# Interleaving the last Exp and Ln halves of a prefix log-sum-exp scan, and storing the tile above the last in two column halves

## The chip, the cores and the metric

The kernel runs on one core of a Trainium2 chip. The metric is the device time in microseconds (us) of one execution of the whole program. Before the change it is 1255.22 us, the median of six executions (1253.7 to 1270.8).

## What is computed

The input `x` has the shape 8 x 4096 x 2048 in float32. Along the middle axis a running log-sum-exp is taken, for each of the 8 batches and each of the 2048 columns by itself:

```
out[:, 0, :] = x[:, 0, :]
for t in range(1, S):
    mx = maximum(out[:, t-1, :], x[:, t, :])
    out[:, t, :] = mx + log(exp(out[:, t-1, :] - mx) + exp(x[:, t, :] - mx))
```

This is log(cumulative sum of exp(x)). Input and output have 268.44 MB each, and every byte crosses between HBM and the core once.

## The kernel before

**Tiles.** The 4096 rows of a batch are cut in 8 blocks (NBLK) of 512 rows, so there are 64 tiles (NT), each of 512 rows x 2048 columns, 4 MB. A tile lies in the core's memory as 128 partitions x 4 rows (R) x 2048 columns: partition p holds the four consecutive rows 4p to 4p+3, which are 32 KB in one piece in HBM. There are four input buffers `ti` and two output buffers `to`. Every tile is worked on in two column halves of 1024 columns, h = 0 and h = 1. Below, "Exp 63/0" is the Exp of tile 63, column half 0, and so on.

**Stages of a tile.** (1) SyncE loads the tile into `ti` (L114). (2) ScalarE takes Exp in place, one instruction for each half (L133). (3) VectorE adds each row of a partition to the one after it, three additions for each half (`local`, L248). (4) TensorE multiplies the last rows with a triangle of ones, which gives each partition the sum of all partitions above it (`triangle`, L224, two matmuls for each half into PSUM). (5) VectorE adds that sum to all four rows (`join`, L257, one instruction for each half). (6) TensorE starts the sum of the next tile from the last row of this one (`carry`, L213, two matmuls for each half); the last tile of a batch has no next one, and only a semaphore is passed on. (7) ScalarE takes Ln (L140), one instruction for each half, which waits for the carry of that half. (8) ScalarE's queue issues the store (L165 in the loop, L177 in the tail).

**The order of the work** is written out by hand for each engine; nothing is scheduled by a planner, and each engine executes its own list in order, waiting on semaphores. VectorE's order for each tile is local/0, local/1, join/0, join/1. TensorE's is triangle/0, triangle/1, carry/0, carry/1. SyncE loads tile n+4 into a buffer once both Ln halves of tile n have been taken from it (`freed`). ScalarE's list is a software pipeline: the Exp halves of tile n stand before the Ln halves of tile n-1. A loop covers tiles 0 to 59. The tail, written out after it (L182 to L198), covers the Exp of tiles 61 to 63 and the Ln and the stores of tiles 60 to 63. In the tail Ln works in place in `ti`, and the store leaves from there. All stores of the tail add to one semaphore, `final`, and the last instruction of ScalarE waits for all of them.

**The place that is changed** is the last turn of that tail (n = 63, so `up` = 62):

```
else:
    ln(up, 0, up - first, True)
    exp(n, 0)
    ln(up, 1, up - first, True)
    finals += store(up)
    exp(n, 1)
```

ScalarE thus executes Ln 62/0, Exp 63/0, Ln 62/1, the store of the whole tile 62, Exp 63/1, and then (L196 to L198) Ln 63/0, store 63/0, Ln 63/1, store 63/1. `exp(n, 0)` first takes the semaphore of the tile's load (L132), and whatever stands behind it on ScalarE waits with it. `store(n, h)` waits until that Ln has completed and issues one DMA; with h given, it moves one column half, whose pieces in HBM are 4 KB (one row of 1024 columns) and not 32 KB.

Of the kernel before, what the change touches and what calls it, by code (L numbers as in the profile page):

```python
# [9 lines left out]
def kernel(  # L10
# [29 lines left out]
    NT = B * NBLK  # L40
# [16 lines left out]
    def half(h):  # L57
        return slice(h * HALF, (h + 1) * HALF)

    def event(engine, waits, updates):  # L60

        engine.add_instruction(mybir.InstEventSemaphore(  # L62
            name=f"I-{nc.next_id()}", engine=engine.engine, ins=[], outs=[],
            sync_info=mybir.SyncInfo(
                on_wait=[mybir.SyncWait(
                    sync_type="semaphore", id=s.num, ant_name=s.name,
                    wait_mode="sem-ge-imm", wait_value=n,
                ) for s, n in waits],
                on_update=[mybir.SyncUpdate(
                    sync_type="semaphore", id=s.num, ant_name=s.name,  # L70
                    update_mode=mode, update_value=n,
                ) for s, mode, n in updates],
            ),
        ))

    def take(engine, s, n):

        event(engine, [(s, n)], [(s, "sem-sub-imm", n)])

    with tc.tile_critical():  # L80
# [12 lines left out]
        with nc.Block() as block:  # L93

            @block.gpsimd
            def _(g):
                g.memset(before[:], 1.0).then_inc(ones, 1)  # L97
                g.memset(last[:], 1.0).then_inc(ones, 1)  # L98
                g.wait_ge(ones, 2)

                g.affine_select(  # L101
                    out=before[:], in_=before[:], compare_op=mybir.AluOpType.is_ge, fill=0.0,
                    base=-1, pattern=[[1, P]], channel_multiplier=-1,
                ).then_inc(shaped, 1)

                g.affine_select(  # L106
                    out=last[:], in_=last[:], compare_op=mybir.AluOpType.is_ge, fill=0.0,
                    base=-(P - 1), pattern=[[0, P]], channel_multiplier=1,
                ).then_inc(shaped, 1)
# [17 lines left out]
            @block.scalar  # L127
            def _(act):
                def exp(n, h, rows=slice(0, R)):
                    t = ti[n % NI]  # L130
                    if h == 0:
                        take(act, loaded[n % NI], 16)  # L132
                    act.activation(  # L133
                        t[:, rows, half(h)], t[:, rows, half(h)], ACT.Exp
                    ).then_inc(exps[h], 1)

                def ln(n, h, turn, in_place=False):
                    if h == 0 and not in_place:
                        take(act, stored[n % NO], 16)
                    act.activation(  # L140
                        (ti[n % NI] if in_place else to[n % NO])[:, :, half(h)],
                        ti[n % NI][:, :, half(h)], ACT.Ln,
                    )._wait_ge(carried[h], turn + 1).then_inc(logs, 1)

                def settle(turns):
                    take(act, carried[0], turns)
                    take(act, carried[1], turns)
                    take(act, logs, 2 * turns)

                for n in range(NO):  # L150
                    act.sem_inc(stored[n], 16)
                take(act, top, 16)
                act.activation(ti[0][:, 0:2, :], ti[0][:, 0:2, :], ACT.Exp)  # L153
                exp(0, 0, slice(2, R))
                exp(0, 1, slice(2, R))
                turns = (NT - 2) // NI
                with act.Fori(0, turns) as j:
                    for n in range(1, NI + 1):
                        exp(n, 0)
                        exp(n, 1)  # L160
                        ln(n - 1, 0, n - 1)
                        ln(n - 1, 1, n - 1)

                        event(act, [(logs, 2 * n)], [(freed, "sem-add-imm", 1)])
                        act.dma_start(  # L165
                            out=o_v[bass.ds(j * NI + (n - 1), 1)][0], in_=to[(n - 1) % NO][:]
                        ).then_inc(stored[(n - 1) % NO], 16)
                    settle(NI)


                first = turns * NI
                finals = 0

                def store(n, h=None):
                    cols = slice(0, D) if h is None else half(h)
                    act.wait_ge(logs, 2 * (n - first) + (2 if h is None else h + 1))
                    act.dma_start(  # L177
                        out=o_v[n][:, :, cols], in_=ti[n % NI][:, :, cols]
                    ).then_inc(final, 16)
                    return 1  # L180

                for n in range(first + 1, NT):  # L182
                    up = n - 1
                    if n < NT - 1:
                        exp(n, 0)
                        exp(n, 1)
                        ln(up, 0, up - first, True)
                        ln(up, 1, up - first, True)
                        finals += store(up)
                    else:  # L190
                        ln(up, 0, up - first, True)
                        exp(n, 0)
                        ln(up, 1, up - first, True)
                        finals += store(up)
                        exp(n, 1)
                for h in range(2):  # L196
                    ln(NT - 1, h, NT - 1 - first, True)
                    finals += store(NT - 1, h)  # L198
                settle(NT - first)
                for n in range(NO):  # L200
                    take(act, stored[n], 16)
                take(act, final, 16 * finals)
# [99 lines left out]
```

The softmax here doesn't subtract the row's maximum and nothing guards it: scores larger than these inputs give would overflow.

## Time and profile before

| what | value |
|---|---|
| median of six executions | 1255.22 us |
| the six, in order of size | 1253.7, 1254.3, 1255.08, 1255.37, 1260.5, 1270.8 us |
| the profiled execution | 1255.33 us |
| its span, first to last instruction | 1253.6 us |
| around the span | 1.7 us |
| VectorE busy | 1023.1 us (82%) |
| ScalarE busy | 913.2 us (73%) |
| TensorE matmuls busy | 651.0 us (52%) |
| bytes moved, mean rate over the span | 536.90 MB, 428 GB/s |
| one Exp or Ln half (L133, L140) | 3.6 us |
| one join half (L257) | 4.4 us |
| one of the three additions of a half (L248) | 1.22 us |

The page gives, for the 40th parts of the span, the busy share of each engine and the mean share and rate of the 16 DMA engines. The timeline lists instructions in order of time (start and duration in us, engine, line, output and input; in brackets the idle time before one and what ended it). "ACTq" and "SPq" are the queues of ScalarE and SyncE; a DMA row there is only its issue. For DMAs the profile gives the time from the start of the issue to the landing, which is the last of the 16 completion steps of that DMA. A table by stretches of time gives the busy time and number of instructions of each engine, the granted TensorE clock, the DMA share and the rate; a DMA packet counts in the stretch in which it starts, with its whole duration, so that a share may be over 1.

### The profile page before, as it was taken

How to read it: one execution, taken by the hardware profiler on the slowest of the kernel's cores; microseconds unless marked ns; L12 is line 12 of the kernel's file. 1: busy time of each engine (PE TensorE's matmuls, PEld its weight loads, DVE VectorE, ACT ScalarE, POOL GpSimd, SP SyncE). 2: the span in 40 equal slices, each digit the busy share in tenths (PEclk: the TensorE clock that was granted, in tenths of full speed). 3: DMA queues.
4: the chain of work that ended last, by engine and by line, in shares of the span. 5: the costliest groups of instructions: out<-in, count | busy, mean ns of one | idle time of the engine just before them, and what ended most of it. 6: DMA issues, size and time to landing. Idle time of an engine off the chain costs nothing. (4 is left out here: it accounts for less than half of the span.)

```text
span 1253.6 us, 3677 instructions
## 1 busy us (share of the span) xinstructions
PE 651.0 (52%) x960; PEld 215.4 (17%) x960; DVE 1023.1 (82%) x512; ACT 913.2 (73%) x258; POOL 1.1 (0%) x8
## 2 busy tenths in 40 slices
PE   2655365553555635645455464565545555455542
PEld 0211121111111211212111121121211111112110
DVE  5999787787887977878778788787887878878774
ACT  5876866777767767676686776867768668677874
POOL 0000000000000000000000000000000000000000
PEclk9898777877778768688687886877878778678795
DMA  9999999999999999999999999999999999999996
GB/s 401 418 435 433 432 430 435 434 433 431 434 435 434 435 431 431 435 434 432 432 434 435 434 435 429 434 434 433 431 434 435 434 434 435 428 435 434 433 431 288
DMA packets 19490, 536.90 MB, mean 428 GB/s; under 512 B 2080, under 2 KB 2080, under 8 KB 3104
## 3 DMA queue, kind: packets, MB, share of 16 engines
q1 hardware_dynamic: 9360, 268.44, 49.7%
q10 hardware_dynamic: 10128, 268.44, 49.7%
q8 instruction: 1, 0.02, 0.0%
q14 instruction: 1, 0.01, 0.0%
HBM read 268.44 MB, written 268.44 MB: 428 GB/s over the span
## 5 line engine op out<-in xcount | busy, mean ns | idle before, releaser
L248 DVE TENSOR_TENSOR ti<-ti 128x1024 f32<-128x1024 f32 x384 | 464.7, 1224 | 208.4 <-ACT ti L133 199.6
L140 ACT ACTIVATE to<-ti 128x4096 f32<-128x4096 f32 x120 | 427.6, 3609 | 248.5 <-ACTq L62 247.5
L257 DVE TENSOR_TENSOR ti<-ti,ps 128x4096 f32<-128x4096 f32 x128 | 560.0, 4417 | 9.1 <-PE ps L224 8.4
L224 PE MATMUL ps<-ti,before 128*128 128x512 f32 x512 | 381.2, 896 | 352.2 <-DVE ti L248 351.4
L133 ACT ACTIVATE ti<-ti 128x4096 f32<-128x4096 f32 (+1 forms) x128 | 452.6, 3582 | 59.8 <-ACTq L62 59.4
L213 PE MATMUL ps<-ti,last 128*128 128x512 f32 x448 | 269.8, 733 | 232.6 <-DVE ti L257 232.6
L224 PEld LDWEIGHTS ps<-ti,before 128*128 128x128 f32 x512 | 129.3, 280 | 618.6 <-DVE ti L248 511.5
L213 PEld LDWEIGHTS ps<-ti,last 128*128 128x128 f32 x448 | 86.1, 213 | 400.2 <-DVE ti L257 333.9
L140 ACT ACTIVATE ti<-ti 128x4096 f32<-128x4096 f32 x8 | 28.7, 3606 | 15.4 <-PEq L62 8.9
L153 ACT ACTIVATE ti<-ti 128x4096 f32<-128x4096 f32 x1 | 3.6, 3616 | 6.6 <-ACTq L62 6.6
L34 ACT ACT_TABLE_LOAD x1 | 1.3, 1283 | 0.8 <-PEq L286 0.8
L101 POOL TENSOR_SCALAR_AFFINE_SELECT before<-before 128x128 f32<-128x128 f32 x1 | 0.3, 294 | 0.1
L106 POOL TENSOR_SCALAR_AFFINE_SELECT last<-last 128x128 f32<-128x128 f32 x1 | 0.3, 294 | 0.0
L97 POOL MEMSET before<- 128x128 f32 x1 | 0.2, 206 | 0.5 <-SPq L80 0.5
L98 POOL MEMSET last<- 128x128 f32 x1 | 0.2, 205 | 0.0
L286 POOL MEMSET const-bfloat16-1.0<- 128x1 bf16 x1 | 0.1, 103 | 0.0
L286 POOL MEMSET const-uint8-127<- 128x1 uint8 x1 | 0.1, 102 | 0.0
L286 POOL MEMSET const-float32-0.0<- 128x1 f32 x1 | 0.1, 100 | 0.3 <-issue 0.3
L286 POOL MEMSET const-float32-1.0<- 128x1 f32 x1 | 0.1, 100 | 0.0
## 6 DMA issues: line engine op xcount, KB each, us to landing
ti<-in_x_dram SPq DMA_DIRECT2D x63, 4096.0 KB, 31.2
out_dram<-to ACTq DMA_DIRECT2D x60, 4096.0 KB, 31.4
out_dram<-ti ACTq DMA_DIRECT2D x3, 4096.0 KB, 21.0
ti<-in_x_dram SPq DMA_DIRECT2D x2, 2048.0 KB, 9.7
out_dram<-ti ACTq DMA_DIRECT2D x2, 2048.0 KB, 7.4
```

The source lines that it names most:

```text
L34: nc.scalar.preload_act_table_set("natural_log_exp_and_others")
L97: g.memset(before[:], 1.0).then_inc(ones, 1)
L101: g.affine_select(out=before[:], in_=before[:], compare_op=mybir.AluOpType.is_ge, fill=0.0, base=-1, pattern=[[1, P]], channel_multiplier= ...
L106: g.affine_select(out=last[:], in_=last[:], compare_op=mybir.AluOpType.is_ge, fill=0.0, base=-(P - 1), pattern=[[0, P]], channel_multiplier=1,
L133: act.activation(t[:, rows, half(h)], t[:, rows, half(h)], ACT.Exp).then_inc(exps[h], 1)
L140: act.activation((ti[n % NI] if in_place else to[n % NO])[:, :, half(h)], ti[n % NI][:, :, half(h)], ACT.Ln,)._wait_ge(carried[h], turn + ...
L153: act.activation(ti[0][:, 0:2, :], ti[0][:, 0:2, :], ACT.Exp)
L213: m = pe.matmul(ps[(k + 1) % 2][:, sl], last[:], ti[k % NI][:, R - 1, sl], start=True, stop=False, skip_group_check=True,)
L224: m = pe.matmul(ps[k % 2][:, sl], before[:], ti[k % NI][:, R - 1, sl], start=k == 0, stop=True, skip_group_check=True,)
L248: a = dve.tensor_add(t[:, r, half(h)], t[:, r - 1, half(h)], t[:, r, half(h)])
L257: dve.tensor_add(t[:, :, half(h)], t[:, :, half(h)], ps[n % 2][:, half(h)].unsqueeze(1).to_broadcast([P, R, HALF]),)._wait_ge(ahead[h], n ...
L286: nc = _bacc.Bacc("TRN2", target_bir_lowering=False, num_devices=1)
```

## The change

In the last turn ScalarE's list becomes Exp 63/0, Ln 62/0, store 62/0, Exp 63/1, Ln 62/1, store 62/1. Exp 63/0 moves ahead of Ln 62/0, and Exp 63/1 ahead of Ln 62/1. The store of tile 62 becomes two stores of a column half each, the first of them ahead of Exp 63/1. The rest of the program is the same; the other turns of the tail issue the same instructions in the same order, and the lists of the other engines do not change.

```diff
                 for n in range(first + 1, NT):
                     up = n - 1
+                    exp(n, 0)
                     if n < NT - 1:
-                        exp(n, 0)
                         exp(n, 1)
-                        ln(up, 0, up - first, True)
-                        ln(up, 1, up - first, True)
-                        finals += store(up)
-                    else:
-                        ln(up, 0, up - first, True)
-                        exp(n, 0)
-                        ln(up, 1, up - first, True)
-                        finals += store(up)
+                    ln(up, 0, up - first, True)
+                    if n == NT - 1:
+                        finals += store(up, 0)
                         exp(n, 1)
+                    ln(up, 1, up - first, True)
+                    finals += store(up, 1 if n == NT - 1 else None)
                 for h in range(2):
                     ln(NT - 1, h, NT - 1 - first, True)
                     finals += store(NT - 1, h)
```

## The prediction

> **What bounds the kernel now.** I read the page first, for its slices.
>
> ```profile
> DMA  9999999999999999999999999999999999999996
> GB/s 401 418 435 433 432 430 435 434 433 431 434 435 434 435 431 431 435 434 432 432 434 435 434 435 429 434 434 433 431 434 435 434 434 435 428 435 434 433 431 288
> ```
>
> For 39 slices the 16 DMA engines are busy at some 433 GB/s, and no engine's work there can shorten the run. Only the last slice (31.3 us) has holes. The edit is in that slice, so what it can win is the holes: at 433 GB/s a slice carries 13.57 MB, at 288 GB/s 9.03 MB; the missing 4.54 MB are 10.5 us. That is an upper bound, and it includes the 2 us after the last byte. Next, the timeline of the tail.
>
> ```profile
> 1207.10 0.35 ACTq L177 DMA_DIRECT2D out_dram<-ti  x1
> ...
> 1213.52 3.62 ACT L140 ACTIVATE ti<-ti 128x4096 f32<-128x4096 f32 x1 [6.45 <-PE ps L213]
> ...
> 1217.04 3.60 ACT L133 ACTIVATE ti<-ti 128x4096 f32<-128x4096 f32 x1
> 1220.55 3.60 ACT L140 ACTIVATE ti<-ti 128x4096 f32<-128x4096 f32 x1
> ...
> 1224.18 0.34 ACTq L177 DMA_DIRECT2D out_dram<-ti  x1
> ...
> 1224.56 3.62 ACT L133 ACTIVATE ti<-ti 128x4096 f32<-128x4096 f32 x1 [0.41 <-ACT ti L140]
> ...
> 1228.21 3.75 DVE L248 TENSOR_TENSOR ti<-ti 128x1024 f32<-128x1024 f32 x3 [3.79 <-ACT ti L133]
> 1231.88 8.74 DVE L257 TENSOR_TENSOR ti<-ti,ps 128x4096 f32<-128x4096 f32 x2
> ...
> 1236.41 3.62 ACT L140 ACTIVATE ti<-ti 128x4096 f32<-128x4096 f32 x1 [8.23 <-PEq L62]
> 1240.06 0.62 ACTq L177 DMA_DIRECT2D out_dram<-ti  x1
> 1240.74 3.62 ACT L140 ACTIVATE ti<-ti 128x4096 f32<-128x4096 f32 x1 [0.72 <-PEq L62]
> 1244.39 0.54 ACTq L177 DMA_DIRECT2D out_dram<-ti  x1
> ```
>
> In order these are: the issue of store 61; Ln 62/0, for whose carry ScalarE idled 6.45 us; Exp 63/0; Ln 62/1; store 62; Exp 63/1; VectorE's three additions of 63/1, which waited 3.79 us for that Exp; its two joins of tile 63; Ln 63/0 and its store; Ln 63/1 and its store. The chain that sets the end is Exp 63/1 -> additions -> joins -> Ln 63 -> stores. Now the transfers: each DMA's time from issue to landing (us, last column), for load 63, stores 61 and 62, and the halves 63/0 and 63/1,
>
> ```profile
> ti<-in_x_dram SPq DMA_DIRECT2D x1, 4096.0 KB, 31.3
> ...
> out_dram<-ti ACTq DMA_DIRECT2D x1, 4096.0 KB, 21.0
> ...
> out_dram<-ti ACTq DMA_DIRECT2D x1, 4096.0 KB, 13.6
> ...
> out_dram<-ti ACTq DMA_DIRECT2D x1, 2048.0 KB, 7.0
> ...
> out_dram<-ti ACTq DMA_DIRECT2D x1, 2048.0 KB, 7.8
> ```
>
> and the table by stretches of 1 us (the last two columns are the DMA share and GB/s):
>
> ```profile
> 1224.00:1225.00 1.00, 0.53 (x1) 0.50 (x2) 0.42 (x1) 0.58 (x2) 0.00 (x0) 0.50 0.00 0
> 1225.00:1226.00 1.00, 1.00 (x2) 0.34 (x1) 0.00 (x0) 1.00 (x1) 0.00 (x0) 0.50 1.22 524
> ...
> 1236.00:1237.00 1.00, 0.00 (x0) 0.00 (x0) 1.00 (x2) 0.59 (x1) 0.00 (x0) 0.50 0.08 33
> ...
> 1241.00:1242.00 1.00, 0.00 (x0) 0.00 (x0) 0.00 (x0) 1.00 (x1) 0.00 (x0) 0.50 0.69 283
> ...
> 1251.00:1252.00 1.00, 0.00 (x0) 0.00 (x0) 0.00 (x0) 0.00 (x0) 0.00 (x0) 0.50 0.66 262
> ```
>
> The landings: store 61 at 1207.10 + 21.0 = 1228.1, store 62 at 1224.18 + 13.6 = 1237.8, the last half at 1244.39 + 7.8 = 1252.2; the span ends 1.4 us later. **One DMA engine of the 16 is late.** No packet starts in 1224-1225, so nearly all engines are through with store 61 by about 1225, yet it lands only at 1228.1. Likewise in 1236-1237 a single packet starts (33 GB/s for 1 us is 33 KB, one partition's 32 KB piece; a share of 0.08 is 1.3 us on one engine of 16), and the landing of store 62 follows it. So one engine is about 3 us behind. Today that is harmless, since all engines then idle until store 63/0 sends its first bytes, at about 1241.3.
>
> **The change part by part.**
>
> *Exp 63/0 ahead of Ln 62/0* adds a wait: it needs load 63, issued at 1177.4 (last start of L114), landed at 1177.4 + 31.3 = 1208.7. ScalarE has issued store 61 by 1207.45, so it waits 1.3 us and runs Exp 63/0 from 1208.8 to 1212.4. Behind it stands Ln 62/0, which its carry held to 1213.5 anyway: 1.1 us to spare, and the 3.6 us of the Exp cost nothing, hidden in the 6.45 us of idle. If the load were later than 1209.9, each further us would delay all that follows on ScalarE. SyncE has no later load that could be held up.
>
> *The rest of ScalarE's list.* Ln 62/0 runs 1213.5 to 1217.1. Store 62/0 follows; the same kind of half (63/0) held ScalarE from 1240.03 to 1240.74, 0.7 us. Exp 63/1 therefore runs 1217.85 to 1221.5, in place of 1224.56 to 1228.2: 6.7 us earlier. Ln 62/1 (carry long done: its two matmuls end by 1216.3) runs 1221.4 to 1225.0, 0.85 us later than before, and store 62/1 is issued at 1225.0.
>
> *VectorE and TensorE.* The joins of tile 62 end at 1214.3, additions 63/0 run at once to 1218.0, additions 63/1 wait for Exp 63/1 and run 1221.5 to 1225.2. Triangle 63/0 has been ready by 1222, triangle 63/1 (3.8 us at the clock of 0.50 granted there) ends at 1229.0 beside join 63/0 (1225.2 to 1229.5). All stays 6.7 us ahead: Ln 63/0 at 1229.7, store 63/0 issued at 1233.4, store 63/1 at 1237.7. If the chain alone set the end, the gain would be 6.7 us.
>
> *The transfers.* Store 62/0 is queued at 1217.1, while store 61 still runs, so the hole at 1224-1225 closes. Store 62/1 is queued at 1225.0, when 62/0 has only begun. What do halves cost? Tile 63, in 4 KB packets, runs from 1241.31 (0.69 of a us before 1242) to 1251.7, 10.4 us; tile 62, in 32 KB packets, takes 8 rounds of 1.22 us (the share of 1.22 is 16 packets a us), 9.75 us. Halving tile 62 thus adds 0.65 us to DMA that becomes the bound. The page "DMA: Bandwidth & Descriptors" of the Trainium skill, "Anatomy of one DMA", speaks against it more strongly: every DMA carries a fixed 2.0 us beside its bytes, an extra 2.0 us for one more store. The trace shows that cost only where nothing is queued behind (63/0: 7.0 us to land, 5.2 of bytes): bytes flow on through the seam of 63/0 and 63/1. I take 0.65; the rule would leave 1.4 us less of the gain.
>
> *The sum.* Engines that are on time finish store 61 at about 1225 and then have two tiles in halves: 1225 + 2 x 10.4 = 1245.8, without a hole, as 63/0's bytes can come from 1233.4 + 1.25 = 1234.7 (1.25 us from issue to first byte, from 1240.06 and 1241.31) and the queue has work until 1235.4. The late engine has no idle time left in which to catch up: landing 1228.1 + 20.8 = 1248.9 against 1252.2. So the last landing comes 3.3 us earlier and not 6.7. The span becomes 1250.3; the profiled execution 1255.33 - 3.3 = 1252.0; and as it lies 0.1 above the median, **1251.9 us** is the forecast against 1255.22.
>
> Here a second rule is weighed. The same page ("Latency and other measured facts") says that two DMA engines are usually slower, but holds this for software-made descriptors alone; here both data queues are "hardware_dynamic". By it there would be no late engine, and the gain would be 1252.2 - 0.45 (from last packet to landing) - 1245.8 = 6.0 us. The row shows one, so I take the row, but whether an execution without the profiler has it no view tells.
>
> **The rivals.**
>
> *No late engine without the profiler* (or one that is later by 1 us only): gain 5 to 6.0, bounded by 6.7 of the chain: about 1249.3 us. For it: the page's rule; against: the trace.
>
> *The late engine takes all.* If it is 6 us behind and not 3, it ends where it does today; the 0.65 us remain: 1255 to 1256. A new wait has about the same result: load 63 landing at 1216.6 uses up the chain's 6.7 us (1209.9 + 6.7). Against both: 31.2 and 31.3 us to landing for the last loads, one like the other. The rule of 2.0 us, with issues that ScalarE's queue holds back because more 4 KB packets are pending than the trace ever shows, would leave part: 1253 to 1254.5.
>
> *4 KB packets are dearer behind a full queue: slower.* Place: the four halves on the late engine, 128 packets. At 10.4 us a tile one costs 163 ns. The break-even is 20.8 + 3.3 = 24.1 us, 188 ns each; at 200 ns the run would end 1.5 us later than today, about 1256.7 us. Against it: the rate in tile 63's rows is steady.
>
> **How the numbers follow.** Late engine as in the trace (gain 2 to 4.5, 1250.7 to 1253.2): 0.60. No late engine: 0.20. All or most taken: 0.14. Dearer packets: 0.06. The predicted time is that of the first. The range of 1247.8 to 1256.0 takes in the first three, with the chain's 6.7 us as the floor (1248.5) and 0.7 us below it, as the lower four of the six executions lie 1.7 us apart; it leaves out the fourth. One per cent is 12.6 us, about what a measurement of this kernel can tell from no change; the hole-filling bound is 10.5 us and the chain's 6.7, so within 1% gets 0.94, and 0.03 on each side is for executions that lie apart, as 1270.8 does among the six.
>
> **What would show it.** Right: Exp 63/0 at about 1208.8 after a short wait; Exp 63/1 at 1217.9; Ln 63/0 at 1229.7; no window under 350 GB/s from 1224 to 1244; then one engine alone at work for some 3 us before the last landing at 1248.9. Wrong: Ln 62/0 later than 1213.6 (the load was late); store issues longer than 0.7 us (pending packets); packets over 170 ns; or all engines ending together, near 1246.

## The result, and the profile after

The changed kernel takes 1251.76 us, the median of 34 executions (1250.59 to 1262.44), against 1254.05 us for the kernel before (71 executions, the six of the beginning among them). The ratio is 0.9978, with a 95% interval of 0.9968 to 0.9988: 2.8 us less, between 1.5 and 4.0. By the medians it is 2.3 us less. The forecast was 3.3 us less and 1251.9 us. The gain lies inside the forecast's range of 2 to 4.5 us. Part of the close agreement of the two absolute times is luck: the six executions of the beginning lay 1.2 us above the median of the many.

The profiled execution of the changed kernel took 1253.45 us (span 1251.7 us), 1.7 us more than its median, and its loop ran late; that has to be kept in mind for absolute times. First the page:

```profile
DMA  9999999999999999999999999999999999999997
GB/s 402 418 434 429 434 430 434 436 434 434 429 436 430 431 436 436 431 429 436 431 430 436 436 435 426 436 435 430 434 435 435 428 435 434 430 435 435 434 428 326
```

Only the last slice is another: 326 GB/s where it was 288; the rest agree within 6 GB/s. The holes there have become smaller. The timeline of ScalarE and VectorE in the tail (start and duration in us, idle time before in brackets):

```profile
1210.49 0.35 ACTq L177 DMA_DIRECT2D out_dram<-ti  x1
1210.98 3.62 ACT L133 ACTIVATE ti<-ti 128x4096 f32<-128x4096 f32 x1 [0.52 <-ACTq L62]
...
1215.44 3.62 ACT L140 ACTIVATE ti<-ti 128x4096 f32<-128x4096 f32 x1 [0.85 <-PE ps L210]
...
1219.09 0.63 ACTq L177 DMA_DIRECT2D out_dram<-ti  x1
1219.77 3.62 ACT L133 ACTIVATE ti<-ti 128x4096 f32<-128x4096 f32 x1 [0.71 <-ACT ti L140]
...
1223.42 3.75 DVE L245 TENSOR_TENSOR ti<-ti 128x1024 f32<-128x1024 f32 x3 [2.08 <-ACT ti L133]
1226.93 0.54 ACTq L177 DMA_DIRECT2D out_dram<-ti  x1
1227.08 8.75 DVE L254 TENSOR_TENSOR ti<-ti,ps 128x4096 f32<-128x4096 f32 x2
...
1231.62 3.62 ACT L140 ACTIVATE ti<-ti 128x4096 f32<-128x4096 f32 x1 [4.73 <-PEq L62]
...
1239.60 0.54 ACTq L177 DMA_DIRECT2D out_dram<-ti  x1
```

Store 61 was issued at 1207.10 us before and is issued at 1210.49 here, so times are best counted from that row. From store 61 to the last store it was 1244.39 - 1207.10 = 37.3 us; it is 1239.60 - 1210.49 = 29.1 us. The chain is 8.2 us shorter, and the run only 2 to 3 us. Part of the difference here is the late loop (3.4 us at store 61); the rest lies behind the last issue. From there to the end of the span it was 1253.6 - 1244.39 = 9.2 us, and it is 1251.7 - 1239.60 = 12.1 us. What happens in these 12 us is best seen in another execution of the same kernel (the run g1 below, span 1250.1 us), whose time of 1251.83 us is about the median. Its stretches of 1 us (last two columns: DMA share and GB/s):

```profile
1233.00:1234.00 1.00, 0.00 (x0) 0.00 (x0) 0.44 (x1) 0.43 (x1) 0.00 (x0) 0.50 0.78 320
...
1244.00:1245.00 1.00, 0.00 (x0) 0.00 (x0) 0.00 (x0) 0.00 (x0) 0.00 (x0) 0.50 0.54 217
1245.00:1246.00 1.00, 0.00 (x0) 0.00 (x0) 0.00 (x0) 0.00 (x0) 0.00 (x0) 0.50 0.12 49
1246.00:1247.00 1.00, 0.00 (x0) 0.00 (x0) 0.00 (x0) 0.00 (x0) 0.00 (x0) 0.50 0.07 29
1247.00:1248.00 1.00, 0.00 (x0) 0.00 (x0) 0.00 (x0) 0.00 (x0) 0.00 (x0) 0.50 0.06 25
1248.00:1249.00 1.00, 0.00 (x0) 0.00 (x0) 0.00 (x0) 0.00 (x0) 0.00 (x0) 0.50 0.02 8
```

The seam between tile 62 and tile 63 (1233-1234) keeps 78% of the engines' time, where the kernel before had about 7 us of near silence (1234.1 to 1241.3). Nearly all engines are through by 1244.5; in 1245-1246 the share of 0.12 is two engines. Then a share of 0.06 to 0.07, which is one engine of 16 (1/16 = 0.0625), goes on alone with six or seven 4 KB packets a us until 1248.3. The program waits for that one engine. The same rows of the changed kernel's own profile have one engine left from about 1247.5 to 1250, and those of the run e1 from 1246 to 1248.3. The seam is not closed in every execution, though: those two profiles fall to 90 and 53 GB/s for a us or more there (1234 to 1236), because their on-time engines were through with tile 62 before store 63/0 sent its first bytes.

### The profile page after: what moved, and what is told of

Same layout as the page of the kernel before. It is cut to its first block, busy times and chain, and to the rows that moved or that the text cites. A ratio compares the mean times of both kernels' runs of the same rounds, so it can differ in the third digit from the quotient of the medians.

```text
span 1251.7 us, 3678 instructions
## 1 busy us (share of the span) xinstructions
PE 646.8 (52%) x960; PEld 213.7 (17%) x960; DVE 1023.2 (82%) x512; ACT 913.3 (73%) x258; POOL 1.1 (0%) x8
## 5 line engine op out<-in xcount | busy, mean ns | idle before, releaser
L210 PE MATMUL ps<-ti,last 128*128 128x512 f32 x448 | 266.4, 725 | 236.9 <-DVE ti L254 236.9
## 6 DMA issues: line engine op xcount, KB each, us to landing
ti<-in_x_dram SPq DMA_DIRECT2D x63, 4096.0 KB, 29.1
out_dram<-ti ACTq DMA_DIRECT2D x4, 2048.0 KB, 12.1
```

The costliest lines, as they stand in the source:

```text
L210: m = pe.matmul(ps[(k + 1) % 2][:, sl], last[:], ti[k % NI][:, R - 1, sl], start=True, stop=False, skip_group_check=True,)
```

## The experiments

The letter of a label is its group. The kernels of one group ran on one chip beside the kernel before (medians there 1253.67 us in e, 1254.18 in f and 1254.29 in g). "Above" and "under" are differences of medians; a ratio to the kernel before stands with its 95% interval of 2 to 3 us to each side, so differences under 2 us are not resolved by it. In the groups e and f the ratios put every run 0.4 to 2 us lower against the kernel before than the medians do.

The profiles give a measure beside the times: from the last issue to the end of the span. It is 9.1 to 9.2 us in the kernel before and in f1, f2, g3, e3, e4 and g2: there the chain sets the end, and the last store is through as soon as it can be. In the changed kernel it is 12.1, 12.9 (g1) and 11.7 us (e1), in e2 12.6 us: 2.5 to 3.7 us in which the program waits for transfers that are queued already. In f3 it is 9.5 us, nearly level.

**e1 and g1: the changed kernel again.**

> The changed kernel once more, as the yardstick of this group. Late-engine theory (the transfers set the end, above all on a DMA engine that lags by some 3 us): 2 to 3.5 us under the kernel before. Chain theory (Exp 63/1 to Ln 63 still sets the end): 6.7 us under it.

> The changed kernel once more, as the yardstick of this group: 2 to 3 us under the kernel before.

e1: 1252.17 us, 1.5 us under, ratio 0.9974 (0.9953 to 0.9994). g1: 1251.82 us, 2.5 us under, ratio 0.9974 (0.9956 to 0.9991). A gain of 6.7 us is excluded by both intervals. These two are the yardsticks of their groups.

**g3: the old chain, 3.6 us longer.**

```diff
                         finals += store(up)
+                        take(act, stored[0], 16)
+                        act.activation(to[0][:, :, half(0)], to[0][:, :, half(0)], ACT.Exp)
                         exp(n, 1)
```

> The kernel before with one more Exp half (on an output buffer that nothing reads any more) between the store of tile 62 and Exp 63/1: 3.6 us on the chain that ends there. Reading of the profile before (the chain alone sets its end): 3.4 to 3.7 us above the kernel before. If the transfers set its end too, under 1 us above it.

Measured: 1257.74 us, 3.45 us above the kernel before (ratio 1.0027, 1.0011 to 1.0044). One us on this chain was one us of the run: in the kernel before, the chain set the end. (In g3, as in f3 and g2 below, the wait for `stored` was moved up from the end of the list, where it is missing in turn.)

**f1 and e4: 2 MB less to store, in the old and in the new kernel.** In f1 tile 62's store becomes that of half 1 alone; in e4 the first of the two half stores is taken out:

```diff
-                        finals += store(up, 0)
                         exp(n, 1)
```

> The kernel before without the store of column half 62/0 (2 MB of the output are left out); the counterpart of the same edit in the changed kernel. Reading of the profile before: all engines idle until tile 63's first bytes, so the chain sets the end and the time stays within 0.7 us of the kernel before. If the transfers set the end there too: up to 5 us under it.

> The changed kernel without the store of column half 62/0: 2 MB of the output are left out, 5 us of transfers. Late-engine theory: the chain becomes the bound, its last half landing 7 us after its issue: 3 to 4.5 us under the changed kernel. Transfers bound, but no late engine without the profiler: 1 to 2 us under it. Chain theory: no difference.

f1: 1254.47 us, 0.3 us above the kernel before (ratio 0.9986, 0.9963 to 1.0009). 5 us of transfers fewer changed nothing by the medians, and the ratio's interval leaves room for part of them; in f1's profile all engines idle from 1236 to 1243, so the chain set the end. e4: 1248.09 us, 4.1 us under e1 (ratio 0.9952, 0.9925 to 0.9978, against 0.9974: 2.8 us by the ratios). The same edit that was worth nothing before is worth 3 to 4 us after: the transfers have become the bound. In e4's profile they are so no longer:

```profile
1232.00:1233.00 1.00, 0.00 (x0) 0.00 (x0) 1.00 (x1) 0.65 (x1) 0.00 (x0) 0.50 0.04 16
...
1234.00:1235.00 1.00, 0.00 (x0) 0.00 (x0) 0.00 (x0) 1.00 (x1) 0.00 (x0) 0.50 0.99 406
...
1244.00:1245.00 1.00, 0.00 (x0) 0.00 (x0) 0.00 (x0) 0.00 (x0) 0.00 (x0) 0.50 0.19 74
```

The late engine moves its last bytes in 1232-1233; all begin tile 63 together near 1234, and all are through by 1244.4, with no packet in any later stretch. Such a pause before tile 63 lets the late engine catch up, as in the kernel before.

**f3 and g2: the new chain, made longer.** Two or three Exp halves, whose results nobody reads, ahead of Ln 63/0 (f3's edit; in g2 both output buffers are taken, and `to[1]`, half 0, is the third):

```diff
+                take(act, stored[0], 16)
                 for h in range(2):
+                    act.activation(to[0][:, :, half(h)], to[0][:, :, half(h)], ACT.Exp)
+                for h in range(2):
                     ln(NT - 1, h, NT - 1 - first, True)
```

> The changed kernel with two more Exp halves (on an output buffer that nothing reads any more) ahead of Ln 63/0: 7.1 us of ScalarE work, of which 4 to 4.7 us fall in its idle time, so Ln 63/0 and both stores of tile 63 come 2.5 to 3.1 us later. Late-engine theory: the late engine has 3.8 to 4 us to spare, so under 1 us above the changed kernel. No late engine without the profiler, or chain theory: 2 to 3 us above it.

> The changed kernel with three more Exp halves ahead of Ln 63/0 (on output buffers that nothing reads any more): 10.6 us of ScalarE work, 4 to 4.7 us of it in idle time, so the stores of tile 63 come 5.9 to 6.6 us later. Late-engine theory: 3 to 4 us of that are to spare, so 2 to 3.5 us above the changed kernel, about the time of the kernel before. Chain theory: 6 us above the changed kernel, 3 to 4 us above the kernel before.

f3: 1252.06 us (ratio 0.9971, 0.9952 to 0.9990), beside ratios of 0.9974 (e1 and g1) for the changed kernel without it. From store 61 to the last store it takes 1243.05 - 1211.10 = 32.0 us, 2.6 more than g1; they cost nothing that can be seen. g2: 1255.67 us, 3.85 us above g1 (ratio 1.0009, 0.9993 to 1.0026; 4.4 us by the ratios). Stores 61 and 63/1 in the timelines of g1 and of g2:

```profile
1207.87 0.35 ACTq L177 DMA_DIRECT2D out_dram<-ti  x1
...
1237.21 0.54 ACTq L177 DMA_DIRECT2D out_dram<-ti  x1
```

```profile
1208.63 0.35 ACTq L177 DMA_DIRECT2D out_dram<-ti  x1
...
1244.77 0.54 ACTq L177 DMA_DIRECT2D out_dram<-ti  x1
```

From store 61 to the last store g1 takes 1237.21 - 1207.87 = 29.3 us and g2 1244.77 - 1208.63 = 36.1 us, so 6.8 us were added and 2.4 to 3 of them were free. The new chain has about 3 us to spare, at the low end of the late-engine theory's 3 to 4.

**e3: only Exp 63/0 ahead.**

```diff
                     ln(up, 0, up - first, True)
-                    if n == NT - 1:
-                        finals += store(up, 0)
-                        exp(n, 1)
                     ln(up, 1, up - first, True)
-                    finals += store(up, 1 if n == NT - 1 else None)
+                    finals += store(up)
+                    if n == NT - 1:
+                        exp(n, 1)
```

> Only Exp 63/0 moves ahead of Ln 62/0; Exp 63/1 stays behind the whole store of tile 62. The chain is then 3.5 us earlier than before, and not 6.7. Late-engine theory: that is about all that the transfers can use, so equal to the changed kernel within 0.7 us. Chain theory: half of the changed kernel's gain, about 1.2 us above it.

1252.41 us, 0.24 us above e1 (ratio 0.9980, 0.9959 to 1.0001). One of the change's moves gives all of the gain that can be told apart. In its profile the on-time engines pause at 1233-1237, only 33 GB/s flow, and all engines end tile 63 together at about 1247.6: chain and late engine come out nearly even there.

**e2: the order alone, tile 62 as one store.**

```diff
                     if n == NT - 1:
-                        finals += store(up, 0)
                         exp(n, 1)
                     ln(up, 1, up - first, True)
-                    finals += store(up, 1 if n == NT - 1 else None)
+                    finals += store(up)
```

> Only the order is changed (Exp 63/0, Ln 62/0, Exp 63/1, Ln 62/1), and tile 62 leaves as one whole store behind Ln 62/1. Exp 63/1 comes 0.7 us earlier than in the changed kernel, but no byte of tile 62 is queued before about 1224 us. Late-engine theory: the late engine is still busy with tile 61 then and loses nothing, and 32 KB packets save 0.3 to 0.65 us: equal to the changed kernel or up to 0.7 us under it. Rival (the early half store brings the gain, by filling the hole at 1224 us): 1.5 us or more above the changed kernel.

1251.72 us, 0.45 us under e1 (ratio 0.9972, 0.9952 to 0.9993). By the medians the rival is out: without an early half store the gain is the same, though in e2's profile the hole stays open (98 to 328 GB/s from 1223 to 1228). The intervals of the ratios alone would not exclude it. e2 beats the kernel before; that it beats the changed kernel is not resolved.

**f2: the halves alone, in the old order.**

```diff
                         ln(up, 0, up - first, True)
+                        finals += store(up, 0)
                         exp(n, 0)
                         ln(up, 1, up - first, True)
-                        finals += store(up)
+                        finals += store(up, 1)
                         exp(n, 1)
```

> Only the stores of tile 62 are split: Ln 62/0, store 62/0, Exp 63/0, Ln 62/1, store 62/1, Exp 63/1, in the old order of Exp and Ln. One more issue on ScalarE and longer ones put Exp 63/1 about 1.1 us later. Chain theory for the old order: 0.7 to 1.3 us above the kernel before. Rival (queueing half a tile earlier is what gains): 1 us or more under it.

1255.09 us, 0.9 us above the kernel before by the medians, but with a ratio of 0.9995 (0.9977 to 1.0013). Its sign is not resolved; by the medians a gain of 1 us or more is unlikely. In its profile Ln 62/0 to Exp 63/1 takes 12.15 us, and 11.04 before: the 1.1 us are on the chain.

**f4: the price of 4 KB packets, in the loop.** Each store of the loop becomes two, a column half each, and the waits on `stored` count 32:

```diff
-                        act.dma_start(
-                            out=o_v[bass.ds(j * NI + (n - 1), 1)][0], in_=to[(n - 1) % NO][:]
-                        ).then_inc(stored[(n - 1) % NO], 16)
+                        for h in range(2):
+                            act.dma_start(
+                                out=o_v[bass.ds(j * NI + (n - 1), 1)][0][:, :, half(h)],
+                                in_=to[(n - 1) % NO][:, :, half(h)],
+                            ).then_inc(stored[(n - 1) % NO], 16)
```

> The changed kernel with all 60 stores of the loop split in two column halves at the place of the whole store, in 4 KB packets: the price of 4 KB packets 60 times over, in the stretch that the transfers bound. By the prediction's 0.65 us for a tile: 39 us above the changed kernel. By the 5.0 us between the landings of the halves of tile 62 in the changed kernel's profile (10.0 us a tile against 9.7): 18 us above. By a fixed 2.0 us for each further DMA: 120 us above. By packets that cost nothing more: no difference.

1319.14 us, 67 us above f3 (ratio to the kernel before 1.0507, 1.0471 to 1.0543): 1.1 us a tile, more than any theory but the fixed 2.0 us, which is out too. Its page gives the queues' shares of its span of 1317.3 us (q1: loads, q10: stores), and the time to landing; the same lines of the kernel before stand behind them:

```profile
q1 hardware_dynamic: 9360, 268.44, 50.5%
q10 hardware_dynamic: 65760, 268.44, 49.6%
...
ti<-in_x_dram SPq DMA_DIRECT2D x63, 4096.0 KB, 15.7
```

```profile
q1 hardware_dynamic: 9360, 268.44, 49.7%
q10 hardware_dynamic: 10128, 268.44, 49.7%
...
ti<-in_x_dram SPq DMA_DIRECT2D x63, 4096.0 KB, 31.2
```

Both queues had 49.7% of 1253.6 us before, 623 us each. The stores took 653.4 us here, 30 us more for 61 more halved tiles: 0.5 us a tile. The loads, whose packets did not change, took 665.2 us, 42 us more, 0.7 us a tile. So 0.5 us is the packets' own price, and the rest is paid by the loads beside them. In the tail no load runs beside tile 62. Its halves moved at 416 GB/s in g1 (1225 to 1233), which is 10.1 us for a tile, 0.35 us more than the prediction's 9.75.

## Why the prediction was right, point by point

*The bound now, and the chain of 6.7 us.* Right. g3 and f1 show that the chain alone set the end. From store 61's issue the chain got shorter by 8.2 us in the changed kernel's profile, by 37.3 - 29.3 = 8.0 in g1 and by 5.3 in e1; 6.7 lies between. Two things move it: carry 62/0 took 3.50 us in the profile before, at a granted clock of 0.65 and 0.50, and 1.98 us in these three (6.7 + 1.5 = 8.2); and in e1 the next point took 3.0 us back.

*"1.1 us to spare" at the new wait.* This step was cut too fine: the spare came from that slow carry in the one profile. With the carry at 1.98 us g1 has none left (Exp 63/0 ends at 1213.1, the carry at 1212.9). e1 shows the case with a late load: there load 63 took 33.9 us to land, as did the median load of that execution,

```profile
ti<-in_x_dram SPq DMA_DIRECT2D x1, 4096.0 KB, 33.9
```

and the timeline of e1 reads

```profile
1206.57 0.35 ACTq L177 DMA_DIRECT2D out_dram<-ti  x1
...
1209.45 1.98 PE L210 MATMUL ps<-ti,last 128*128 128x512 f32 x4 [2.35 <-DVE ti L254]
...
1210.87 3.62 ACT L133 ACTIVATE ti<-ti 128x4096 f32<-128x4096 f32 x1 [4.34 <-ACTq L62]
...
1214.40 3.60 ACT L140 ACTIVATE ti<-ti 128x4096 f32<-128x4096 f32 x1
```

The carry for Ln 62/0 was done at 1211.4, but Ln 62/0 started at 1214.4, behind an Exp that had waited 4.34 us for its load. The moved wait cost 3.0 us there, and yet e1's profiled execution took 1251.90 us: the 3 us disappeared in what the chain has to spare. The rival of the new wait was real, and too small to decide.

*The late engine.* Right. g1 has most engines through at 1244.5 and the last one at 1248.3; the forecast had the others at 1245.8, and the landing at 1248.9. In the changed kernel's own profile and in e1 the last engine is some 3 us behind most of the others as well. That it is one engine in the executions whose rows are not shown, no view tells. But their times speak for about 3 us of late transfers: without them the forecast was a gain of 5 to 6.0 us, and the interval ends at 4.0; the added work of f3 would have cost 2 to 3 us and cost nothing; and e4's 4.1 us (2.8 by the ratios) are more than the 1 to 2 us expected (the intervals of f3 and e4, each by itself, do not settle it). The lag is not a constant, and not always that of one engine: at the seam of f2's profile shares of 0.38 to 0.21 (1235 to 1240) are six to three engines, which were still at work some 5 us after the rest. Why an engine lags stays open.

*The signs.* In g1 they came as forecast within 0.8 us: Exp 63/0 at 1209.6 after a wait of 1.7 us, Exp 63/1 at 1217.4, Ln 63/0 at 1229.2, one engine alone at the end. One did not: there were windows under 350 GB/s (320 at 1233 in g1, far less in the changed kernel's own profile and in e1). The forecast had the transfers without a hole; the hole did no visible harm, since in all three some engine was at work through it and ended last. And one sign of being wrong came, Ln 62/0 held up by the load, in e1.

*The halves of tile 62 at 0.65 us.* Somewhat too large: 0.5 us by f4, 0.35 by the rate in g1. The 0.65 was taken from tile 63, which moved more slowly (406 GB/s in the kernel before, 1242 to 1251, against 416 for tile 62); why stays open. The fixed 2.0 us of the Trainium skill's page "DMA: Bandwidth & Descriptors" ("Anatomy of one DMA") is fitted there to DMAs issued from GpSimd, whose descriptors software writes, so the prediction took the rule further than the page does. It was not paid here, where the next DMA is queued behind: 60 further DMAs cost 67 us in f4, not 120, and the stores' own share was 30.

*The sum.* 3.3 us forecast, 2.8 us by the ratio and 2.3 by the medians; 3.3 is inside the interval. The change makes the chain 5 to 8 us shorter, and 3 to 5 us of that are lost because the late engine now goes from tile to tile without a pause: the pause was its time to catch up. The rivals "chain alone" (6.7 us), "no late engine" (5 to 6.0), "all taken" (nothing) and "dearer packets" (slower) are out by the interval of 1.5 to 4.0. The "rule of 2.0 us" (0.7 to 2.2 us left) is not out by it, but by f4.

## What to carry to other kernels

At the end of a transfer-bound kernel, work out two ends: that of the chain of work, and that of the queued bytes on the slowest DMA engine; a shorter chain is worth only the distance between them, here about 3 of 5 to 8 us. A pause of the transfers costs time, but it also let the engine that lagged come level (e3, e4, g2), so closing it gave back less than its length. Moving an instruction that waits for a load ahead of others puts all of them behind that load; take its spare from several executions: in these profiles carry 62/0 took 1.98 to 3.61 us, and load 63 landed 29.0 to 33.9 us after its issue.

## What the runs showed of the hardware that was not expected

Smaller packets in one queue changed the other. With stores in 4 KB packets (f4) the loads, still in 32 KB packets, landed in 15.7 us instead of 31.2, and their packets' own time rose by 7% (665 against 623 us). From 720 to 730 us, with both queues at work, f4's trace has 115 packets of the loads and 120 of the stores, and the loads had 85% of the engines' time. The Trainium skill ("DMA: Bandwidth & Descriptors", "Queues, rings and completion order") says that an engine takes turns between its queues packet by packet, which fits: a 32 KB packet against a 4 KB one. Why the loads' packets took longer stays open. And at the end of a run of 1250 us one DMA engine of 16, in some executions several, was some 3 us or more behind the rest, on queues that the profile calls hardware_dynamic. The landing times that the profile gives for the tail's stores need care: all add to one semaphore, so with four in flight the 16th step that is counted need not be that store's own.
